# A hybrid SSM and latent-attention decoder layer: attention's weight splits and gates on GpSimd, weights loaded two ahead, and three moves around them

## The chip, the cores and the metric

The kernel runs on one NeuronCore of a Trainium2 chip. The metric is the device time in microseconds (us) of one execution; the median of several runs counts. Five engines work side by side, each through its own queue in order: TensorE (PE: matmuls, and the loads of their stationary operand, PEld), VectorE (DVE), ScalarE (ACT), GpSimd (POOL) and SyncE (SP, which only starts DMAs here). They wait for one another through semaphores.

## The reference, cut to what matters

One layer for 512 tokens of width 1024. Parallel head groups read the same normalised input through one input projection, one output projection mixes them, and an expert mixer (PEER) follows:

```python
proj = h @ w_in
z, xbc, dt_raw, q_lat, kv_lat, k_pe = jnp.split(proj, ...)
xbc = jax.nn.silu(causal_dwconv(xbc, conv_w, conv_b))
...
y_ssm = rms_norm(y.reshape(B, S, SSM_WIDTH) * jax.nn.silu(z), ssm_norm_g)
y_mla = mla_heads(q_lat, kv_lat, k_pe, cos, sin, q_norm_g, w_q_b, kv_norm_g, w_kv_b)
mix = jnp.concatenate([y_ssm, y_mla], axis=-1) @ w_out
...
h = layer_norm(DEEPNORM_ALPHA * h + mix, ln_mix_g, ln_mix_b)
ffn = peer(h, w_query, sub_keys, u_table, v_table)
```

The SSM heads (16, Mamba-2) work in chunks with decays exp(a_cum[l] - a_cum[s]). The latent attention has 8 heads of 128 unrotated and 64 rotated dimensions, and is causal. PEER picks 16 of 16384 experts for each token and head.

## The kernel before, in words

**Precision and the weight stream.** Nearly every product is made of three fast matmuls: each operand is split into a high part (rounded) and a low part (the rest), and `mm3` (L71 to L74) adds high by high (L72), high by low (L73) and low by high (L74). The weights come through one `Stream` called `win` (L80 to L127, made in L263): a list of items in the order of use, each at most 128 x 1024. `loads` starts the DMA of an item on SP into one of three raw buffers (tile `wir`); `his` makes the high part on ACT (L109, `wih`); `splits` makes the low part by a subtraction (L119, `wil`) on the engine that `lo_on[0]` names at that moment, and then asks for the raw load three items on. `get(n)` sees to it that items up to n + `win.la` are split: `la` is how many weights ahead the stream runs. There are three buffers of each part. Engines take their instructions in the order in which this program issues them, so where a split is issued decides what stands behind it.

**Stages.** (1) Input layer norm: statistics on DVE, normalising on ACT and DVE, transposes on PE (L311) into the eight tiles `PS8`, from which ACT and DVE make the split input HH and HL (L317 to L322). (2) Input projection, 18 column blocks (L592 to L616 and L657 to L669), and behind it the convolutions: `conv_a` (taps on DVE, L376 to L378), `conv_b` (Silu on ACT, L387), `conv_c` (transposes on PE, L396, and evacuation on ACT, L401). `ssd_a` (L478) makes eight exponentials of decays on ACT (L482) and multiplies them on DVE by the chunk's products (L483); `ssd_y` (L512) uses them and `xdt` (L494) in matmuls (L518). The list `work` (L618) lays the remaining SSM steps behind the later column blocks and the z projection (L672 on). (3) Attention, below. (4) The output projection for three token blocks (L1218 on), the mixing layer norm, the query projection (L953) with the top-16 searches on DVE, during which `lo_on[0]` is GpSimd, and the expert stage to the end.

**Attention (L857 to L901).** Ahead of the loop: `q_pe(0)` and `qk_nope(0)` in halves, then two halves of `chain(qk_nope(1), v_proj(0))`; a half ends at a `yield`. `q_pe` (L727) projects the rotated dimensions of a pair of heads: 9 matmuls, evacuation to `qx` on ACT (L734), a split of the next item, `yield`; then the permuting matmul (L738), the rotation on DVE (`rope`, L578 to L580), its halves (L742, L743) and four DMAs on GpSimd's queue (L746). `qk_nope` and `v_proj` (L770, L749) have two halves each and ask for the next split after a half. The loop has 39 steps; step st works for head st // 4 and query block st % 4: `p_scale` (two steps late; DVE L818, or ACT L816 for the longer rows of heads below 7), `scores` (PE, and the maximum on DVE, L800), `p_tr` (six steps late: transposes on PE, L827, evacuated as two halves by ACT, L721, and DVE, L722), one half of the projections (`next(g)`), from step 28 the output projection of the fourth token block (`w_out_step`, one item a step), `p_exp` (ACT, L808), `gate` in steps 1, 3, 5 and 7, and `p_v` (seven steps late). `gate(c, 1)` multiplies 512 columns of the SSM output by silu(z) on DVE (L541) and squares them on ACT (L543); `gate(c, 0)` runs earlier, from `work`. `win.la` is 0 in the loop up to step 27, so that only the explicit `win.splits(cnt[0] + 1)` run ahead; 1 from step 28; 2 once the output projection's first step has been issued.

Of the kernel before, what the change touches and what calls it, by code (L numbers as in the profile page):

```python
# [17 lines left out]
AF = mybir.ActivationFunctionType  # L18
OP = mybir.AluOpType
# [6 lines left out]
NB = 4  # L26
# [3 lines left out]
SCALE = 192.0 ** -0.5  # L30
# [23 lines left out]
def tile_block(ctx: ExitStack, tc: tile.TileContext, I, out):  # L54
    nc = tc.nc
    ctx.enter_context(tc.manual_schedule())
    V, A, T, G = nc.vector, nc.scalar, nc.tensor, nc.gpsimd
# [83 lines left out]
    def sqrt_rs(p, v, shape, tag, eps):  # L141
        h, q, y, a = (p.tile(shape, F32, name=tag + n) for n in "hqya")
        A.activation(q, v, AF.Sqrt, bias=eps)
        V.tensor_scalar(h, v, EPS, -0.5, op0=OP.add, op1=OP.mult)
        V.reciprocal(y, q)
        V.tensor_tensor(a, y, y, op=OP.mult)
        V.tensor_tensor(a, a, h, op=OP.mult)
        V.scalar_tensor_tensor(y, a, 1.5, y, op0=OP.add, op1=OP.mult)
        return y
# [76 lines left out]
    zt = zx.tile([128, NB, D], F32, name="zt")  # L226
    xs = [zx.tile([128, NB, 512], F32, name=f"xs{e}") for e in range(2)]
# [7 lines left out]
    ones = wk.tile([128, 128], F32, name="ones")  # L235
# [12 lines left out]
    lo_on = [V]  # L248
# [14 lines left out]
    win = Stream(wst, "wi", items, [128, 1024], raw=3, la=2, lo=lambda n: lo_on[0])  # L263
    cnt = [0]
# [22 lines left out]
    w0 = lnp.tile([128, 1], F32, name="w0")  # L287
    A.activation(w0, ones[:, 0:1], AF.Sqrt, bias=eps)
    PS8 = [pa() if k < 4 else pb() for k in range(8)]
    for p in range(2):  # L290
        bs = slice(2 * p, 2 * p + 2)
        for b in (2 * p, 2 * p + 1):
            st6 = lnp.tile([128, 2, 6], F32, name="st6", bufs=2)
            for i in range(2):
                V.bn_stats(st6[:, i], XH[:, b, i * 512:(i + 1) * 512])
            V.bn_aggr(mv4[:, b], st6.rearrange("p a b -> p (a b)"))
        nm = lnp.tile([128, 2], F32, name="nm", bufs=2)
        rs = sqrt_rs(lnp, mv4[:, bs, 1], [128, 2], f"l{p}", eps)
        V.scalar_tensor_tensor(nm, mv4[:, bs, 0], -1.0, rs, op0=OP.mult, op1=OP.mult)
        if p:  # L300
            win.his(1)
        for j, cs, act in (((0, slice(0, D), 1), (1, slice(0, D), 1)) if p == 0 else
                           ((0, slice(0, D), 0), (1, slice(0, 512), 1), (1, slice(512, D), 0))):
            t = XH[:, 2 * p + j, cs]
            if act:
                A.activation(t, t, AF.Identity, bias=nm[:, j:j + 1], scale=rs[:, j:j + 1])
            else:
                V.tensor_scalar(t, t, rs[:, j:j + 1], nm[:, j:j + 1], op0=OP.mult, op1=OP.add)
        for k in range(8):
            for b in (2 * p, 2 * p + 1):  # L310
                T.transpose(PS8[k][:, b * 128:(b + 1) * 128], XH[:, b, k * 128:(k + 1) * 128], ident)  # L311
    win.his(2)
    win.splits(1)
    for k in range(8):
        ht = lnp.tile([128, S], F32, name="ht", bufs=3)
        pl, pg = PAR[:, P_LB + k:P_LB + k + 1], PAR[:, P_LG + k:P_LG + k + 1]
        A.activation(ht, PS8[k], AF.Identity, bias=pl, scale=pg)  # L317
        if k % 2:
            A.activation(HH[:, k], PS8[k], AF.Identity, bias=pl, scale=pg)
        else:  # L320
# [37 lines left out]
    def proj(i):  # L358
        if i < 2:
            return two[i]  # L360
        hl = item()
        ps = pa()
        for k in range(8):
            proj_k(ps, hl, k)
        return ps
# [24 lines left out]
    def conv_c(i):  # L390
        o = co.pop(i)
        if i in (3, 4):
            return
        ps = pb()
        for c in range(NB):
            T.transpose(ps[:, c * 128:(c + 1) * 128], o[:, c * 128:(c + 1) * 128], ident)  # L396
        pv = ps.rearrange("p (c t) -> p c t", c=NB)
        if i <= 2:
            A.activation(btok[:, :, i - 1, :], pv, AF.Copy)
        else:  # L400
            A.activation(xs[(i - 5) // 4][:, :, (i - 5) % 4 * 128:((i - 5) % 4 + 1) * 128], pv, AF.Copy)  # L401
# [76 lines left out]
    def ssd_a(c, g):  # L478
        de = de_[c * 2 + g]
        for h in range(8):  # L480
            hh = g * 8 + h
            A.activation(de[:, h], de[:, h], AF.Exp, bias=nac[:, c, hh:hh + 1])  # L482
        V.tensor_tensor(de, de, SD["cb"][:, g:g + 1].to_broadcast([128, 8, 128]), op=OP.mult)  # L483

    def ssd_m(c, g):
        de = de_[c * 2 + g]
        V.tensor_tensor(de, de, ntm[:, None, :].to_broadcast([128, 8, 128]), op=OP.add)
# [38 lines left out]
    def ssd_s(c):  # L526
# [9 lines left out]
                A.activation(nxt[:, g * 512:(g + 1) * 512], pS, AF.Copy)  # L536
        prev[0] = nxt

    def gate(c, e):
        es = slice(e * 512, (e + 1) * 512)  # L540
        V.tensor_tensor(xs[e][:, c], xs[e][:, c], zt[:, c, es], op=OP.mult)  # L541
        t = wk.tile([128, S], F32, name="co", bufs=2) if e == 0 else ml.tile([128, S], F32, name="rp")
        A.activation(t, xs[e][:, c], AF.Square, accum_out=ssq[:, c, e:e + 1])  # L543

# [47 lines left out]
    for i in range(13):  # L592
        ps = proj(i)
        if i == 0:
            A.activation(kd[0:80], ps[0:80], AF.Copy)
        else:
            conv_a(i, ps)
        if i >= 2:
            conv_b(i - 1)
        if i >= 5:  # L600
            conv_c(i - 2)
        if i in (4, 5):
            conv_c(i - 3)
        if i in (2, 4, 6, 7, 9):
            next(dp)
        if i == 3:
            k_rope()
        if i == 11:
            ssd_m(0, 0)
        if i == 12:  # L610
            ssd_cb(0)
            ssd_m(0, 1)
            ssd_a(0, 0)
    conv_b(12)
    conv_c(11)
    ssd_a(0, 1)  # L616

    work = {0: [(conv_c, 12), (ssd_x, 0), (ssd_cb, 1), (ssd_m, 1, 0)],  # L618
# [38 lines left out]
    for i in range(13, 18):  # L657
        ps = proj(i)
# [68 lines left out]
    def q_pe(p):  # L727
        wh, wl = item()
        ps = pp()
        for k in range(3):  # L730
            ks = slice(k * 128, k * 128 + 128)
            mm3(ps, wh[:, ks], wl[:, ks], qlh[:, k], qll[:, k], k == 0, k == 2)
        qx = ml.tile([128, S], F32, name="qx")
        A.activation(qx, ps, AF.Copy, scale=SCALE)  # L734
        win.splits(cnt[0] + 1)
        yield
        pr = pp()
        T.matmul(pr, C[:, C_PQ:C_PQ + 128], qx, start=True, stop=True)  # L738
        a = rope(ml, qx, pr, "rp", 1)
        q2 = [ml.tile([128, S], F32R, name=f"q2{e}", bufs=2) for e in range(2)]  # L740
        qp = [ml.tile([128, S], F32R, name="qp" + n) for n in "hl"]
        A.activation(qp[0], a, AF.Copy)  # L742
        V.tensor_tensor(qp[1], a, qp[0], op=OP.subtract)  # L743
        for e in range(2):
            for x in (e, 1 - e):
                G.dma_start(q2[e][x * 64:x * 64 + 64], qp[e ^ x][e * 64:e * 64 + 64])  # L746
            QP[2 * p + e] = q2[e]
# [110 lines left out]
    for g in (gq, gk, gq, gk, gk):  # L858
        next(g, None)
    g = chain(qk_nope(1, pq=pt), v_proj(0))  # L860
    for _ in range(2):
        next(g)
    acc3 = {}
    win.la = 0
    for st in range(39):
        h, q = divmod(st, 4)
        if st == 28:
            win.la = 1
        if q == 0 and h:
            g = iter(())  # L870
            if h < 7:
                g = chain(qk_nope(h + 1), v_proj(h // 2)) if h % 2 == 0 else chain(q_pe(h // 2 + 1), qk_nope(h + 1))
        if 1 < st < 34:
            p_scale((st - 2) // 4, (st - 2) % 4)
        if st < 32:
            scores(h, q)
        if 6 <= st < 38:
            p_tr((st - 6) // 4, (st - 6) % 4)
        if GST[3] + 10 <= st < GST[3] + 18:
            y_tr(st - GST[3] - 10)  # L880
        next(g, None)
        if st >= 28:
            if st == 28:
                acc3 = {(3, e): pu() for e in range(2)}
            if st < 36:
                w_out_step(acc3, (3,), st - 28)
            elif st == 37:
                w_out_step(acc3, (3,), 8)
        if st < 32:
            p_exp(h, q)  # L890
        if st in GST:
            gate(GST.index(st), 1)
        if GST[3] < st <= GST[3] + 8:
            if st == GST[3] + 1:
                g2 = gate2()
            next(g2)
        if st == GST[3] + 8:
            ZH = zx.tile([128, NB, D], F32R, name="zt")
        if st >= 7:
            p_v((st - 7) // 4, (st - 7) % 4)  # L900
# [317 lines left out]
    acc = {(b, e): px() if b == 0 else pw() for b in range(3) for e in range(2)}  # L1218
    for k in range(10):
        w_out_step(acc, (0, 1, 2), k)  # L1220
        win.la = 2
        if k == 1:
            V.memset(one, 1.0)
            V.memset(scl, 1.0)
            rows(ROW, 2)
            nc.sync.dma_start(ident, I["idn"])
            for b in range(3):
                load_h(b)
# [101 lines left out]
    for m in range(17):  # L1330
# [9 lines left out]
        while tm[1] < tm[0] + T_Q:  # L1340
            c = next(fill, None)
# [340 lines left out]
```

## Time and profile before

| what | us |
|---|---|
| median of 3 runs (lowest, highest) | 1615.43 (1614.64, 1615.7) |
| the profiled execution | 1614.06 |
| its span, first to last instruction | 1612.3 |
| PE busy in the span | 1580.4 |
| DVE busy | 1356.4 |
| ACT busy | 711.2 |
| POOL busy | 470.3 |

All times of the trace count from the span's start. In these times the start and layer norm end at about 17, the input projections and the SSM steps at 201, attention at 340, the output projection for three blocks at 400, and the expert stage runs to the end. A group's row gives line, engine, operation, what is written from what is read, shapes and count, busy time and mean ns of one, then the idle time of the engine just before them and what ended it. A wait row gives who waited for whom, in total, how often, and the longest. The chain of waits is the work that ended last, followed back from the end: start, length, what. The end of a matmul is modelled, so PE's busy time is an upper bound.

### The profile page before, as it was taken

Reading aid. Unit: us, or ns where it says so; the run is one execution under the profiler, and the core shown is the slowest. Engines: PE = TensorE matmul, PEld = TensorE weight load, DVE = VectorE, ACT = ScalarE, POOL = GpSimd, SP = SyncE. Lnnn points to the kernel's source line nnn. Section 1 sums busy time; section 2 is a strip of 40 time slices with the busy share of each in tenths; the row PEclk is TensorE's granted clock in tenths of the full one; section 3 lists DMA queues with packets and bytes.
Section 4 is the critical chain, followed back from the end, with each engine's and each line's share of the span. In section 5 each row is a group of like instructions: output and inputs, shape, how many; then the busy total and the mean of one; then the engine's idle time right before and its main releaser. Section 6 shows DMA issues by size and latency. Waiting matters only on the chain.

```text
span 1612.3 us, 23768 instructions
## 1 busy us (share of the span) xinstructions
PE 1580.4 (98%) x8643; PEld 1391.4 (86%) x8643; DVE 1356.4 (84%) x2548; ACT 711.2 (44%) x1236; POOL 470.3 (29%) x340
## 2 busy tenths in 40 slices
PE   7999999999999999999999999999999999999997
PEld 5877878778888999999999999999999999888886
DVE  8979667746799999999488888888889888999877
ACT  5574467632433445556444333333334333333332
POOL 0000010000133223100045555555555555644400
PEclk9999999999999999999999999999999999999999
DMA  6242122374332458777689999999999999999973
GB/s 247 97 153 92 46 71 57 110 239 153 122 100 85 127 183 328 285 256 250 210 311 369 343 343 343 362 347 343 350 348 346 352 344 361 357 346 347 342 221 125
DMA packets 152254, 395.43 MB, mean 245 GB/s; under 512 B 12776, under 2 KB 65720, under 8 KB 150344
## 3 DMA queue, kind: packets, MB, share of 16 engines
q1 hardware_dynamic: 104952, 213.19, 39.3%
q0 software_dynamic: 43584, 155.29, 26.4%
q10 hardware_dynamic: 3600, 25.43, 4.2%
q8 instruction: 68, 1.11, 0.3%
q14 instruction: 50, 0.41, 0.1%
HBM read 359.99 MB, written 31.78 MB: 243 GB/s over the span
## 4 chain that ended last, share of the span: by engine, by line
PE 81%; DVE 13%; ACT 3%; issue 1%; DMA 1%; ACTq 0%; DVEq 0%; POOL 0%
PE va L1429 11%; PE va L1433 11%; PE va L1430 10%; PE pu L72 10%; PE pu L73 10%; PE pu L74 10%; PE pa L73 3%; PE pa L74 3%; PE pa L72 3%; DVE t L987 1%; PE pw L73 1%; PE pw L74 1%; DVE wil L119 1%; PE pw L72 1%; PE pw L1189 1%; PE pw L1190 1%
## 5 line engine op out<-in xcount | busy, mean ns | idle before, releaser
L109 ACT ACTIVATE wih<-wir 128x1024 fp32r<-128x1024 f32 (+2 forms) x269 | 278.0, 1034 | 299.9 <-DMA wir<-ut 104.5
L119 DVE TENSOR_TENSOR wil<-wir,wih 128x1024 fp32r<-128x1024 f32 (+1 forms) x254 | 302.4, 1191 | 102.6 <-ACT wih L109 56.9
L74 PE MATMUL pu<-XTH,wil 128*128 128x368 f32 x1008 | 331.8, 329 | 1.0 <-DVE wil L119 0.9
L72 PE MATMUL pu<-XTH,wih 128*128 128x368 f32 x904 | 299.9, 332 | 0.3 <-ACT act L1271 0.3
L73 PE MATMUL pu<-XTL,wih 128*128 128x368 f32 x904 | 296.8, 328 | 0.0
L1430 PE MATMUL va<-wil,Ph 128*128 128x512 f32 x726 | 282.7, 389 | 0.0
L1467 POOL DMA_INDIRECT row<-u,ix x128 | 185.3, 1448 | 250.8 <-DVE row L1478 128.6
L1467 POOL DMA_INDIRECT row<-v,ix x128 | 188.5, 1472 | 174.8 <-DVE ac L1484 149.2
L74 PEld LDWEIGHTS pu<-XTH,wil 128*128 128x128 f32 x1008 | 189.1, 188 | 1.7 <-DVE wil L119 1.6
L72 PEld LDWEIGHTS pu<-XTH,wih 128*128 128x128 f32 x904 | 169.7, 188 | 3.4 <-ACT act L1271 0.5
L73 PEld LDWEIGHTS pu<-XTL,wih 128*128 128x128 f32 x904 | 169.5, 188 | 2.9
L1429 PE MATMUL va<-wih,Ph 128*128 128x512 f32 x432 | 168.5, 390 | 0.0
L1484 DVE SCALAR_TENSOR_TENSOR ac<-row,hd,ac 128x1024 f32<-128x1024 f32 x128 | 164.1, 1282 | 3.2 <-DMA row<-v,ix 1.0
L1430 PEld LDWEIGHTS va<-wil,Ph 128*128 128x128 f32 x726 | 136.2, 188 | 25.9
L1478 DVE SCALAR_TENSOR_TENSOR row<-row,x 128x1024 f32<-128x1024 f32 x128 | 150.1, 1220 | 1.0 <-DMA row<-u,ix 0.9
L109 ACT ACTIVATE wihx<-wir 128x1024 fp32r<-128x1024 f32 x67 | 71.1, 1062 | 154.2 <-DMA wir<-v 132.4
L1433 PE MATMUL va<-wih,Pl 128*128 128x512 f32 x432 | 133.4, 390 | 0.0
L1271 ACT ACTIVATE act<-pu 128x368 f32<-128x368 f32 x126 | 59.9, 475 | 165.4 <-PE pu L74 165.2
L1429 PE MATMUL va<-wihx,Ph 128*128 128x512 f32 x294 | 114.8, 391 | 0.0
L119 DVE TENSOR_TENSOR wil<-wir,wihx 128x1024 fp32r<-128x1024 f32 x62 | 75.8, 1223 | 43.2 <-issue 32.5
L1433 PEld LDWEIGHTS va<-wih,Pl 128*128 128x128 f32 x432 | 81.1, 188 | 17.3
L1429 PEld LDWEIGHTS va<-wih,Ph 128*128 128x128 f32 x432 | 81.2, 188 | 15.7
(494 smaller groups left out, 3064.7 us busy)
## 6 DMA issues: line engine op xcount, KB each, us to landing
wir<-ut SPq DMA_DIRECT2D x128, 512.0 KB, 6.2
wir<-v SPq DMA_DIRECT2D x128, 512.0 KB, 6.6
gsp<-stg ACTq DMA_DIRECT2D x12, 1920.0 KB, 7.5
gt<-gsp SPq DMA_DIRECT2D x30, 768.0 KB, 10.2
wir<-wo SPq DMA_DIRECT2D x26, 512.0 KB, 4.1
wir<-wf SPq DMA_DIRECT2D x18, 512.0 KB, 3.3
wir<-wqr SPq DMA_DIRECT2D x16, 512.0 KB, 3.6
de<-acd POOLq DMA_DIRECT2D x8, 512.0 KB, 5.1
```

Of the source, the lines that this page charges most:

```text
L72: T.matmul(ps, lh, rh, start=start, stop=False)
L73: T.matmul(ps, lh, rl, start=False, stop=False)
L74: T.matmul(ps, ll, rh, start=False, stop=stop)
L109: A.activation(h, r, AF.Copy)
L119: self.lo(n).tensor_tensor(l, r, h, op=OP.subtract)
L1271: A.activation(ACT[c][:, :NU], ps, AF.Gelu)
L1429: T.matmul(va[b][e], Ph[:, bs], h[:, cs], start=c == 0, stop=False)
L1430: T.matmul(va[b][e], Ph[:, bs], l[:, cs], start=False, stop=False)
L1433: T.matmul(va[b][e], Pl[:, bs], h[:, cs], start=False, stop=c == 127)
L1467: G.indirect_dma_start(out=R[s], out_offset=None, in_=I["u"] if s < 128 else I["v"], in_offset=bass.IndirectOffsetOnAxis(ap=ix[:, s % 128: ...
L1478: V.scalar_tensor_tensor(r, r, 1.0, x3, op0=OP.mult, op1=OP.mult, accum_out=hd[:, s:s + 1])
L1484: V.scalar_tensor_tensor(ac, r, hd[:, s - 128:s - 127], ac, op0=OP.mult, op1=OP.add)
```

## The change

1. 28 matmuls of 128 x 128 ones into the last of the eight `PS8` tiles, ahead of the first transposes.
2. The SSM decays' first eight exponentials, `ssd_a(0, 0)`, are issued after the last convolution's Silu instead of before it.
3. The multiplication of `gate(c, 1)` goes to GpSimd; all four are issued ahead of the attention loop. The squares on ACT stay where they were.
4. `q_pe` evacuates `qx` on DVE for the pairs after the first.
5. A third half, the first of `v_proj(0)`, is issued ahead of the loop.
6. The low parts of weights are made on GpSimd from the loop's beginning to step 34, on DVE from step 35.
7. Weights run two ahead from step 28 (at step 27 two items are asked for), and stay so into the output projection.

```diff
     PS8 = [pa() if k < 4 else pb() for k in range(8)]
+    for _ in range(28):
+        T.matmul(PS8[7][:, 0:128], ones, ones, start=True, stop=True)
     for p in range(2):
...
+    def gate_mul(c, e, eng):
+        eng.tensor_tensor(xs[e][:, c], xs[e][:, c], zt[:, c, e * 512:(e + 1) * 512], op=OP.mult)
+
     def gate(c, e):
-        es = slice(e * 512, (e + 1) * 512)
-        V.tensor_tensor(xs[e][:, c], xs[e][:, c], zt[:, c, es], op=OP.mult)
+        if e == 0:
+            gate_mul(c, e, V)
...
             ssd_m(0, 1)
-            ssd_a(0, 0)
     conv_b(12)
     conv_c(11)
+    ssd_a(0, 0)
     ssd_a(0, 1)
...
         qx = ml.tile([128, S], F32, name="qx")
-        A.activation(qx, ps, AF.Copy, scale=SCALE)
+        if p:
+            V.tensor_scalar(qx, ps, SCALE, None, op0=OP.mult)
+        else:
+            A.activation(qx, ps, AF.Copy, scale=SCALE)
...
     g = chain(qk_nope(1, pq=pt), v_proj(0))
-    for _ in range(2):
+    for _ in range(3):
         next(g)
+    for c in range(NB):
+        gate_mul(c, 1, G)
     acc3 = {}
     win.la = 0
+    lo_on[0] = G
     for st in range(39):
         h, q = divmod(st, 4)
         if st == 28:
-            win.la = 1
+            win.la = 2
+        if st == 35:
+            lo_on[0] = V
...
         next(g, None)
+        if st == 27:
+            win.splits(cnt[0] + 2)
...
         w_out_step(acc, (0, 1, 2), k)
-        win.la = 2
```

## The prediction, made before the changed kernel was run

> **What bounds the kernel now.** I read first how busy each engine is by stage (columns: stage, its length, then busy time and instructions of PE, PEld, DVE, ACT, POOL, granted clock, DMA share, GB/s), and beside it one matmul group of the page (count, busy, mean ns, idle before).
> ```profile
> 201.00:340.00 139.00, 130.43 (x740) 106.89 (x739) 103.39 (x221) 92.14 (x201) 8.19 (x16) 1.00 0.34 96
> 590.00:1590.00 1000.00, 999.69 (x5663) 903.04 (x5662) 859.45 (x1061) 418.99 (x698) 401.38 (x280) 1.00 0.90 320
> ```
> ```profile
> L1430 PE MATMUL va<-wil,Ph 128*128 128x512 f32 x726 | 282.7, 389 | 0.0
> ```
> TensorE (PE) is the bound: in the long expert stage from 590 to 1590 it is idle 0.3 us. The change touches the start, the stretch around 100 us and the attention stage, 201 to 340, where PE is idle 8.6 of 139 us. All later work hangs on attention's result, so a microsecond won there moves the end by one. VectorE (DVE) works 103.4 us of that stage: not full, yet a queue in strict order, and PE waits for what stands late in it. So next I read who PE waits for (total us, times, longest), from 0 to 400.
> ```profile
> PE pa L311 <- ACT XH L306: 10.3, 2, 9.6
> PE pu L73 <- DVE wil L119: 1.7, 4, 0.8
> PE pt L827 <- DVE thl L722: 1.5, 2, 1.0
> PE pt L796 <- DMA q<-qpl: 1.4, 1, 1.4
> PE po L73 <- DVE thl L722: 1.0, 2, 0.7
> PE px L73 <- DVE wil L119: 0.8, 1, 0.8
> PE pt L567 <- DVE thl L722: 0.7, 1, 0.7
> PE pu L738 <- ACT qx L734: 0.7, 1, 0.7
> PE pb L518 <- PE pa L74: 0.7, 1, 0.7
> PE pb L396 <- ACT co L387: 0.7, 2, 0.4
> PE po L72 <- ACT thh L721: 0.7, 1, 0.7
> ```
> L311 is the start, L518 and L396 lie around 100 us. The other rows sum to 8.5, all of attention's idle time: 2.5 for split weights (wil), 3.9 for the probabilities' two halves (L721, L722), 1.4 for the rotated queries' DMA, 0.7 for qx. Ends of matmuls are modelled: 5663 in 999.69 us start 0.18 us apart, while 512 columns are given 389 ns. So each of these 14 waits can hide another 0.16, some 2.2 us in all (an estimate).
>
> **The change part by part.** *Warm-ups (after L289).* The transposes at the start:
> ```profile
> 12.29 1.92 PE L311 MATMUL pb<-ident,XH 128*128 128x128 f32 x8
> ...
> 15.20 1.04 PE L311 MATMUL pb<-ident,XH 128*128 128x128 f32 x8
> ```
> ```profile
> 14.67 1.45 ACT L317 ACTIVATE ht<-pa,PAR 128x512 f32<-128x512 f32 x2 [0.45 <-PE pa L311]
> ```
> Eight take 1.92 us, a later eight of the same 1.04: PE is slow at first. 28 such matmuls cost at most 28 x 0.24 = 6.7 us and wait for one memset, so they fit into PE's first wait of 9.6; if they didn't, each would push the transposes by 0.24. If the transposes then run fast, L317 starts earlier by its idle 0.45 at most, since ACT converts a weight until then. Bounds 0 and -0.45; I take **-0.4**, by the later eight. The Trainium skill (TensorE: Matmul & The Clock Gate, part 1) has the array at half clock again after an idle window of some 3.4 us. The gap here would be about 3, so by the page the gain could go either way, and no run here shows such a gap.
>
> *Exponentials behind the convolutions* (DVE's last convolution; then ACT's queue):
> ```profile
> 96.34 2.33 DVE L378 SCALAR_TENSOR_TENSOR ca<-cu,PAR,ca 128x512 f32<-128x512 f32 x3
> ```
> ```profile
> 97.01 1.28 ACT L482 ACT_TABLE_LOAD   x1
> 98.30 2.46 ACT L482 ACTIVATE de<-de,nac 128x128 f32<-128x128 f32 x8
> 100.77 1.28 ACT L387 ACT_TABLE_LOAD   x1
> ...
> 103.20 1.28 ACT L482 ACT_TABLE_LOAD   x1
> 104.50 2.46 ACT L482 ACTIVATE de<-de,nac 128x128 f32<-128x128 f32 x8
> ```
> Now: exp, Silu, exp, with three table loads. Afterwards Silu comes first and needs no load, but waits for its convolution, to 98.67. From the end of the second load to that of Silu and L401 are 103.20 - 102.05 = 1.15 us; with one load and sixteen exponentials, 98.67 + 1.15 + 1.28 + 4.92 = 106.0 against 106.96. The product and split that DVE owes to L518 come 0.9 sooner, and L396 finds its tile 3 us sooner. Bounds 0 and -1.4 (both rows); **-1.0**.
>
> *Third projection half in front.* Twelve 256-column matmuls move ahead of PE's wait for the query DMA; with their evacuation they are now steps 0's and 1's work, so nothing is added. At 0.18 us or less each they cover most of the 1.4. Bounds 0 and -1.4; **-1.2**.
>
> *Splits, gates and qx.* DVE's splits from 205 to 340, ACT's conversion ahead of them, GpSimd's rate in the query stage, and a landing time from the page:
> ```profile
> L119 DVE TENSOR_TENSOR wil<-wir,wih 128x1024 fp32r<-128x1024 f32 x14 | 17.2, 1226 | 6.4 <-ACT wih L109 6.1
> ```
> ```profile
> L119 DVE TENSOR_TENSOR wil<-wir,wih 128x640 fp32r<-128x640 f32 x6 | 4.9, 820 | 4.1 <-ACT wih L109 4.1
> ```
> ```profile
> L109 ACT ACTIVATE wih<-wir 128x1024 fp32r<-128x1024 f32 x14 | 14.8, 1054 | 3.6 <-DMA wir<-wo 2.2 <-DVE wil L119 1.3
> ```
> ```profile
> L119 POOL TENSOR_TENSOR wil<-wir,wih x15: 2385/2398/2415, 427.5 to 539.7; 128x1024 fp32r<-128x1024 f32 x15
> ```
> ```profile
> wir<-wo SPq DMA_DIRECT2D x26, 512.0 KB, 4.1
> ```
> Where they reach PE, from the chain of waits:
> ```profile
> 221.28 0.48 ACT qx L734
> 221.76 0.63 ACT wih L109
> ```
> ```profile
> 227.56 0.73 DVE wil L119
> 228.29 0.60 DVE xs L541
> ```
> Up to step 35, nine of the wide splits move (w_out 0 to 8), all six of 640 columns, three of 512 and two of 384 (by columns 0.66 and 0.49), and four gates (0.60): 11.0 + 4.9 + 2.0 + 1.0 + 2.4 = 21.3 us leave DVE. Three qx come to it, by columns 0.66 each: 19.3 net. On GpSimd, 2.40 for 1024 columns makes 1.50, 1.20, 0.90 and 1.20 a gate by columns (bounds: that, and 2.40 each): 21.6 + 9.0 + 3.6 + 1.8 + 4.8 = 41 us in 125. Its queue also issues the rotated queries' DMAs, in which it waits for ACT; the next weight behind them is used three steps later.
>
> *qx (0.7):* on DVE it no longer stands behind ACT's squares. But the weight that ACT converts behind it is used one step later; GpSimd takes 1.50 for it instead of 0.82 and starts 0.48 sooner, so it comes 0.2 later, three times. Bounds -0.7 and +2.0 (3 x 0.68); **-0.5**, nearer to the row. *Probabilities (3.9):* at 227.56 a split and a gate, 1.3 us, stand in DVE's queue ahead of a tile that PE wants; gone, that wait goes. Other waits have one split ahead, or softmax work alone. Bounds 0 and -3.9; **-2.5**. *w_out's weights (2.5):* two ahead takes most, but three raw buffers turn over in 4.1 + 1.05 + 2.40 = 7.55 us, and three fast steps now take 7.33, from the first to the last of four splits:
> ```profile
> 317.73 1.23 DVE L119 TENSOR_TENSOR wil<-wir,wih 128x1024 fp32r<-128x1024 f32 x1
> ...
> 325.06 1.23 DVE L119 TENSOR_TENSOR wil<-wir,wih 128x1024 fp32r<-128x1024 f32 x1 [0.26 <-ACT wih L109]
> ```
> Bounds 0 and -2.5; **-2.0**. Of the hidden 2.2 a third: **-0.8**.
>
> *The price: DVE and GpSimd at once.* The query stage has one place that shows it.
> ```profile
> L1003 DVE TENSOR_TENSOR cand<-tv x24: 199/254/1872, 442.0 to 543.2; 128x64 f32<-128x64 f32 x8, 128x96 f32<-128x96 f32 x8, 128x192 f32<-128x192 f32 x8
> ```
> ```profile
> 497.40 2.39 POOL L119 TENSOR_TENSOR wil<-wir,wih 128x1024 fp32r<-128x1024 f32 x1 [3.96 <-PE pw L74]
> 498.00 2.31 DVE L1003 TENSOR_TENSOR cand<-tv 128x64 f32<-128x64 f32 x3
> ```
> A sum of two SBUF operands whose median is 0.25 lasts up to 1.87: it stands until GpSimd's split ends. In attention the DVE operations on SBUF alone that remain are 18 scalings (L818), four of L560 and six of the rotations (L578, L743): 28. GpSimd is busy a third of the time, so 9 are hit, each by half a split, about 1.0: 9 us back on a queue that lost 19.3, of which PE waits for a tenth, as it now waits 8.5 us for a DVE stage of 103. Bounds 0 and +8.7 (28 hit, less 19.3); **+1.0**. The Trainium skill (SBUF — State Buffer, "Who interferes with whom") has such DVE instructions and a GpSimd instruction that reads SBUF exclude each other for a whole instruction. The row agrees; it is the rule against this change.
>
> Sum: -0.4 - 1.0 - 1.2 - 0.5 - 2.5 - 2.0 - 0.8 + 1.0 = **-7.4**. The profiled execution took 1614.06 (span 1612.3, and 1.8 around it): 1606.7. The median of the runs stands 1.37 above it, so I predict **1608.0**.
>
> **The rivals.** *All waits go:* -0.45 - 1.4 - 8.5 - 2.2 = -12.5, 1602.9. For it: DVE loses a fifth of its work. Against: some probability waits lie behind softmax work.
> *Late weights:* the three tight splits cost 0.68 each and qx stays in the way by what they take (+1.4 in all); the raw buffers keep w_out's waits (0); ACT, waiting in order for raw weights, halves the probabilities' gain (-1.2) and the hidden one (-0.4). With -2.6 from the first three terms and +1.0: -1.8, 1613.6. For it: 7.55 against 7.33, and DVE's idle 4.1 before the 640-wide splits: they start as soon as ACT is done, so nothing can be had by an earlier start. Against: two weights of lead. The Trainium skill (GPSIMD Engine Reference, 2.1) gives some 6 us for a first call after a kernel is loaded; that would hold the first gate, ACT's square behind it and this weight by a microsecond or two, and no row here shows such a load's price.
> *The lock* (slower): all 28 hit, since splits and scalings both follow ACT; DVE's queue is then 8.7 longer, and once its relief is spent PE waits for all of it: +8.7 - 2.6 = +6.1, 1621.5. It decides from about 19 hits; a third of 28 is 9.
>
> **How the numbers follow.** Forecast 0.58, all waits 0.14, late weights 0.19, the lock 0.09. A measurement can tell some 0.2% from no change, 3.2 us, so faster is below 1612.2: forecast, all waits and 0.02 of late weights, 0.74; same 0.17, slower 0.09. The range runs from under the second case to beyond the third, 1602.5 to 1616.0; the lock and the outer tails, under 0.2, stay out.
>
> **What would show it.** L796's DMA wait under 0.3; two table loads fewer between 95 and 107 and no L518 wait; eight transposes in about 1 us from the first; no waits of PE for wil; POOL some 41 us busier in attention, DVE 19 less plus the lock's share, which shows as longer L818 and L578; PE's idle 8.6 down to about 3. I am wrong if PE waits for wil on POOL, if the 28 lengthen by a microsecond each, or if idle time turns up after 340.

## The result, and the profile after

| | before | after |
|---|---|---|
| median, us (lowest, highest; 5 runs each, same chip) | 1614.64 (1613.85, 1615.7) | 1604.77 (1604.7, 1605.71) |
| the profiled execution | 1614.06 | 1604.7 |
| its span | 1612.3 | 1602.9 |

The ratio of the times is 0.9939, with a 95% interval of 0.9925 to 0.9954: 9.9 us faster, where 7.4 was forecast. (The time of before in the table ahead of the prediction comes from other runs.) As a time, 1608.0 was forecast: of the 3.2 us by which the measured one lies below it, some 2.5 are the change, and some 0.8 the kernel before, whose median was 1615.43 in the runs that the forecast started from. Lines of the kernel after stand 2 to 8 below those of before, and 14 in the expert stage: L313 is the old L311, L520 the old L518, L542 the gate product (L541), L552 and L565 the old L547 and L560, L727 the low part (L722), L740 and L742 qx on DVE and on ACT, L804 the old L796, L816 the exponential (L808), L826 the scaling (L818) and L835 the transposes of probabilities (L827).

To find where the time went I took the start of the same PE matmul in both traces and subtracted. Such a number is called a **shift** below. It falls in six steps:

| by (us in the trace of before) | shift | what lies there |
|---|---|---|
| 20 | -0.47 | first transposes |
| 200 | -1.30 | the exponentials near 100 us |
| 217.3 | -2.74 at the first scores, -1.32 behind them | third half in front: won, and given back |
| 224 | -2.07 | second pair's qx |
| 302 | -6.10 | the softmax steps |
| 340 | -9.50 | w_out's steps in the loop |
| 1590 | -9.36 | everything behind |

Attention in the changed kernel begins at about 200 and ends 9.5 sooner than before, at 330.5. Its busy time by engine (stage, length, then PE, PEld, DVE, ACT, POOL, granted clock, DMA share, GB/s):

```profile
201.00:332.00 131.00, 127.50 (x741) 107.03 (x741) 97.64 (x201) 89.67 (x194) 48.93 (x39) 1.00 0.37 105
```

PE is idle 3.5 us of it, where it was 8.6. Idle time fell by 5.1, yet the stage got 9.50 - 1.30 = 8.2 shorter, so 3.1 us stood in no idle row: by this subtraction they lay under the modelled ends of matmuls. The softmax steps and w_out's steps, the same work before and after:

```profile
224.00:302.00 78.00, 74.00 (x446) 61.92 (x444) 60.54 (x144) 53.88 (x127) 6.13 (x12) 1.00 0.27 70
302.00:340.00 38.00, 35.54 (x186) 28.35 (x186) 28.50 (x48) 24.62 (x44) 0.00 (x0) 1.00 0.55 171
```

```profile
221.93:295.90 73.97, 72.56 (x446) 61.67 (x444) 55.68 (x132) 52.92 (x124) 20.09 (x22) 1.00 0.27 71
295.90:330.50 34.60, 33.84 (x186) 28.44 (x186) 22.89 (x39) 24.87 (x44) 21.74 (x9) 1.00 0.61 184
```

PE's idle time falls from 4.0 to 1.4 and from 2.5 to 0.8, by 4.3 in all, and the two get 4.0 and 3.4 shorter. Whom PE still waits for, 0 to 400 us (total, times, longest):

```profile
PE pt L72 <- ACT P L816: 1.2, 1, 1.2
...
PE pt L572 <- DVE thl L727: 0.9, 1, 0.9
...
PE pt L835 <- DVE P L826: 0.4, 1, 0.4
PE pb L520 <- DVE xdt L496: 0.4, 1, 0.4
...
PE pb L398 <- ACT co L389: 0.4, 1, 0.4
PE pt L835 <- DVE thl L727: 0.4, 1, 0.4
PE pu L72 <- DVE vl L727: 0.3, 1, 0.3
...
PE po L73 <- DVE thl L727: 0.2, 1, 0.2
```

The reader is to see what is missing: the DMA wait of 1.4, qx's 0.7 and all the waits for split weights (wil, 2.5). Of 3.9 for the probabilities' halves (thl, thh), 0.9, 0.4 and 0.2 are left. New in attention are small rows for a scaling (0.4) and a value's low part (0.3), and the first: PE waits 1.2 for the softmax's exponential.

The start of PE's timeline (start, length, engine, line, operation, count, idle before):

```profile
1.07 9.25 PE L291 MATMUL pb<-ones 128*128 128x128 f32 x56 [1.07 <-DVE eps L285]
10.16 0.27 PE L313 MATMUL pa<-ident,XH 128*128 128x128 f32 x1
10.84 0.98 PE L313 MATMUL pa<-ident,XH 128*128 128x128 f32 x7 [0.41 <-ACT XH L308]
11.66 1.04 PE L313 MATMUL pb<-ident,XH 128*128 128x128 f32 x8
```

The 28 warm-ups are 56 records and take 9.25 us. They even push the first transpose from 9.62 to 10.16, which costs nothing, as the second has to wait for ACT until 10.84. From there all run at the fast rate. Near 100 us, ACT's timeline has one table load in place of three:

```profile
99.41 1.28 ACT L484 ACT_TABLE_LOAD   x1
100.70 4.80 ACT L484 ACTIVATE de<-de,nac 128x128 f32<-128x128 f32 x16
```

It ends at 105.5, where the working had 106.0 and the kernel before 106.96. GpSimd's groups in attention (count, busy, mean ns of one, idle before) and two of VectorE's:

```profile
L119 POOL TENSOR_TENSOR wil<-wir,wih 128x1024 fp32r<-128x1024 f32 x9 | 21.7, 2434 | 7.7 <-PE pt L805 5.0 <-ACT wih L109 2.7
L119 POOL TENSOR_TENSOR wil<-wir,wih 128x640 fp32r<-128x640 f32 x5 | 7.9, 1578 | 11.2 <-ACT wih L109 11.2
L542 POOL TENSOR_TENSOR xs<-xs,zt 128x512 f32<-128x512 f32 x4 | 5.0, 1306 | 0.1
```

```profile
L119 DVE TENSOR_TENSOR wil<-wir,wih 128x640 fp32r<-128x640 f32 x2 | 6.1, 3053 | 0.3 <-ACT wih L109 0.3
L826 DVE TENSOR_SCALAR P<-P,sm 128x256 f32<-128x256 f32 x8 | 3.6, 453 | 0.3
L565 DVE TENSOR_SCALAR xs<-xs,rqy 128x512 f32<-128x512 f32 x4 | 3.1, 776 | 0.0
```

Only five of the six 640-column splits went to GpSimd. The sixth stayed on VectorE, in a row with one from before 204 us, and their mean is 3053 ns where it had been 820. That is the most telling row of the trace, and it leads to the new wait. VectorE, GpSimd and ScalarE at that place:

```profile
209.43 5.28 DVE L119 TENSOR_TENSOR wil<-wir,wih 128x640 fp32r<-128x640 f32 x1
214.63 0.68 DVE L727 TENSOR_TENSOR vl<-pu,vh 128x512 fp32r<-128x512 f32 x1
215.24 0.28 DVE L808 TENSOR_REDUCE mx<-pt 128x1 f32<-128x128 f32 x1
```

```profile
208.98 5.04 POOL L542 TENSOR_TENSOR xs<-xs,zt 128x512 f32<-128x512 f32 x4
```

```profile
212.55 1.28 ACT L816 ACT_TABLE_LOAD   x1
215.55 0.37 ACT L816 ACTIVATE P<-pt,mx 128x128 f32<-128x128 f32 x1 [1.72 <-DVE mx L808]
```

One split of 640 columns stands for 5.28 us while GpSimd's four gate products run back to back, and ends 0.69 us after them (209.43 + 5.28 = 214.71, against 214.02). Behind it in VectorE's queue stand the value's low part and the first maximum; for the maximum waits the exponential, and for that PE.

### The profile page after: what moved, and what is told of

Read it like the earlier page. It is cut to its first block, busy times and chain, and to the rows that moved or that the text cites. A ratio compares the mean times of both kernels' runs of the same rounds, so it can differ in the third digit from the quotient of the medians.

```text
span 1602.9 us, 23887 instructions
## 1 busy us (share of the span) xinstructions
PE 1585.0 (99%) x8699; PEld 1398.6 (87%) x8699; DVE 1349.6 (84%) x2528; ACT 707.2 (44%) x1231; POOL 527.6 (33%) x363
## 4 chain that ended last, share of the span: by engine, by line
PE 89%; DVE 6%; ACT 3%; DMA 1%; issue 1%; DVEq 0%; ACTq 0%
PE pu L72 11%; PE va L1443 11%; PE va L1447 11%; PE va L1444 11%; PE pu L74 10%; PE pu L73 10%; PE pw L73 3%; PE pw L74 3%; PE pw L72 3%; PE pa L73 3%; PE pa L74 3%; PE pa L72 3%; PE pw L1204 1%; PE pw L1205 1%; PE pb L520 1%
## 5 line engine op out<-in xcount | busy, mean ns | idle before, releaser
L119 DVE TENSOR_TENSOR wil<-wir,wih 128x1024 fp32r<-128x1024 f32 (+1 forms) x235 | 288.3, 1227 | 94.4 <-ACT wih L109 63.7
L1481 POOL DMA_INDIRECT row<-u,ix x128 | 196.3, 1533 | 240.9 <-DVE row L1492 118.9
L1481 POOL DMA_INDIRECT row<-v,ix x128 | 194.1, 1516 | 167.5 <-DVE ac L1498 143.6
L119 POOL TENSOR_TENSOR wil<-wir,wih 128x1024 fp32r<-128x1024 f32 (+3 forms) x34 | 71.5, 2108 | 192.4 <-PE pw L74 140.9
L119 DVE TENSOR_TENSOR wil<-wir,wihx 128x1024 fp32r<-128x1024 f32 x62 | 75.8, 1222 | 34.3 <-issue 18.5
```

Of the source, the lines that this page charges most:

```text
L119: self.lo(n).tensor_tensor(l, r, h, op=OP.subtract)
L1481: G.indirect_dma_start(out=R[s], out_offset=None, in_=I["u"] if s < 128 else I["v"], in_offset=bass.IndirectOffsetOnAxis(ap=ix[:, s % 128: ...
```

## The experiments

The theory to be tested: **the lock** holds a VectorE instruction with two SBUF operands until GpSimd's run of instructions is over. In front of the loop it takes back what the third half wins. The rest of the gain is made by the engine that splits and by the lead of two weights. Rivals: the front's wait comes from the table load or from the order on ScalarE; the lead alone, or the engine alone, makes the gain behind it. Each kernel is the changed one with the edit given, except for `starts_alone`, which is the kernel before with two edits. Its runs are compared with the kernel before on the same chip (medians 1614.67, 1614.8 and 1614.73 in the three sets of runs).

Shifts against the kernel before, in the profiled executions:

```
                  200 us  217.4    224     302     340    1590   median us
after              -1.30  -1.34  -2.07   -6.10   -9.50   -9.36   1604.77
front_on_g         -1.33  -2.75  -3.50   -7.49  -10.67  -10.45   1605.25
front_again        -1.35  -2.77  -3.51   -7.52  -10.79  -11.08   1603.8
two_gates          -1.36  -2.78  -3.54   -6.06   -9.48   -8.89   1605.17 (one run)
two_halves         -1.32  -1.31  -1.61   -5.63   -8.99   -5.79   1605.24
gates_on_dve       -1.30  -2.69  -3.44   -5.86   -9.05   -9.08   1604.99
ahead_dve          -1.24  -1.28  -2.01   -4.78   -7.86   -6.58   1606.75
one_ahead          -1.33  -1.37  -2.09   -6.12   -0.05   +5.59   1614.13
qx_on_act          -1.30  -1.34  -1.17   -5.09   -7.84   -3.36   1605.69
starts_alone       -1.35  -1.30  -1.31   -1.35   -1.38   -0.92   1613.23
warm_14            -0.79  -0.80  -1.53   -5.49   -8.85   -8.15   1605.9 (one run)
front_and_scale    -1.36  -2.78  -3.53   -7.54  -10.96  -10.89   1603.2
```

Between 340 and 1590 some executions lose 1 to 6 us that others of the same kernel don't. In the profiled one of `two_halves` (1608.3, where the four others took 1605.02 to 1605.6) it is a wait in the expert stage:

```profile
PE va L1443 <- ACT Ph L1427: 2.1, 1, 2.1
```

So what an edit does to attention is read from the shift at 340, and its time from the median.

**front_on_g: the split in front goes to GpSimd.**

```diff
-    for _ in range(3):
+    for i in range(3):
+        if i == 2:
+            lo_on[0] = G
         next(g)
```

> Edit: the 640-column split that the third projection half asks for goes to GpSimd, ahead of its four gate products, and is not on VectorE any more. Theory (the lock): VectorE's 5.28 us instruction was held by GpSimd's four products that ran back to back; with the split in GpSimd's own queue no VectorE split stands there, vl and mx start some 4 us sooner, PE's wait of 1.2 us on ACT's exponential goes, and the third half keeps its 1.42 us: 1604.8 - 1.4 = 1603.4. Rival (late weight): the split takes 1.58 us on GpSimd instead of 0.82, the products and ACT's square come behind it, and the first query half or the first scores wait instead: 0 to -0.7, 1604.1 to 1604.8, and the row of vl and mx moves by less than 2 us.

Measured: 1605.25 us (1603.25 to 1610.36, six runs; ratio 0.9944, 0.9932 to 0.9956). VectorE and GpSimd at the place of the lock:

```profile
210.19 0.69 DVE L727 TENSOR_TENSOR vl<-pu,vh 128x512 fp32r<-128x512 f32 x1 [0.72 <-ACT vh L726]
210.80 0.28 DVE L808 TENSOR_REDUCE mx<-pt 128x1 f32<-128x128 f32 x1
212.55 0.69 DVE L727 TENSOR_TENSOR vl<-pu,vh 128x512 fp32r<-128x512 f32 x1 [1.47 <-ACT vh L726]
...
214.52 0.33 DVE L826 TENSOR_SCALAR P<-P,sm 128x128 f32<-128x128 f32 x1
```

```profile
209.45 1.56 POOL L119 TENSOR_TENSOR wil<-wir,wih 128x640 fp32r<-128x640 f32 x1 [0.59 <-ACT wih L109]
210.98 5.04 POOL L542 TENSOR_TENSOR xs<-xs,zt 128x512 f32<-128x512 f32 x4
```

The first maximum comes at 210.80 instead of 215.24, 4.4 sooner, as the lock theory said and the rival denied; PE's row of 1.2 is gone, and the shift at 224 is -3.50 against -2.07: 1.43 won. At 340 there are 1.17 of it left. The first vl stands beside GpSimd's split, the second, at 212.55, beside the products. Both read PSUM and last 0.69 as ever: they are not held. The scaling at 214.52 has all its operands in SBUF and starts beside the third product; it ends at 214.85, 0.08 after that product and 1.2 before the fourth is over, so it isn't held for the run. The mechanism is shown for the split; the time, by these six runs, is not.

**front_again: the same kernel on another chip.**

> Edit: the kernel front_on_g once more, on a chip where two others are timed beside it. Theory (its trace keeps 1.1 to 1.2 of the 1.4 at the end, and executions near 1605.3 have a late wait of some 2 us that has nothing to do with the edit): the lowest executions stand at 1603.3 to 1603.6, the lowest of the three kernels without the other edit. Rival (the earlier start makes the late wait more frequent): half or more of the executions stand at 1605 or above again, and the median is no better than 1604.8.

Measured: 1603.8 us (1603.01 to 1605.14, five runs; ratio 0.9935, 0.9921 to 0.9948), shift -10.79 at 340. Of eleven executions in all, six lie between 1603.0 and 1603.8, four between 1605.1 and 1605.6, and one at 1610.36. The theory holds for six of them; why five are later isn't settled, since the two profiled ones are among the six.

**two_gates: two gate products in front instead of four.**

```diff
-        if e == 0:
+        if e == 0 or c > 1:
             gate_mul(c, e, V)
...
-    for c in range(NB):
+    for c in range(2):
         gate_mul(c, 1, G)
```

> Edit: two of the four gate products go to GpSimd in front, the other two to VectorE at their old places in the loop. Theory (VectorE's split is held until GpSimd's run of instructions is over): the row falls with the length of the run, from 5.28 to about 5.28 - 2 x 1.3 = 2.7 us, and PE's wait on ACT's exponential of 1.2 to 0. Rival (the two share the port and the split is merely slowed, by 5.28 / 0.82 = 6.4 while both run): the split does 2.6 / 6.4 = 0.4 of its work beside two products and the rest alone, 2.6 + 0.49 = 3.1 us; or the length has nothing to do with the products: 5.28 as before.

Measured:

```profile
209.38 2.82 DVE L119 TENSOR_TENSOR wil<-wir,wih 128x640 fp32r<-128x640 f32 x1
```

```profile
208.93 2.58 POOL L542 TENSOR_TENSOR xs<-xs,zt 128x512 f32<-128x512 f32 x2
```

2.82 instead of 5.28. More telling than the length is the end: VectorE's instruction ends at 212.20, 0.69 after GpSimd's run at 211.51, the same 0.69 as with four products. Had it been only slowed, more of it would have been done beside the longer run. It is held until the run is over, and is not let in between two instructions of the run. PE's 1.2 is gone here too (shift -3.54 at 224). Behind the front, though, this kernel wins only 2.5 up to 302, where the changed kernel wins 4.0; what is lost there is told under `gates_on_dve`.

Such a hold to the end of a run isn't found for every pair. Late in the changed kernel's attention VectorE scales probabilities, with one operand from SBUF, beside a run of splits:

```profile
311.32 2.18 DVE L826 TENSOR_SCALAR P<-P,sm 128x384 f32<-128x384 f32 x1
```

```profile
310.88 9.78 POOL L119 TENSOR_TENSOR wil<-wir,wih 128x1024 fp32r<-128x1024 f32 x4 [0.87 <-ACT wih L109]
```

The scaling ends at 313.50. One split takes 2.4, so it waited for the first of the four, to 313.3, and not for the run. The scaling at 214.52 in `front_on_g` was not held for the run either, and there GpSimd's run is the very one, four gate products without a wait, that holds the split in the changed kernel. So the difference seems to lie in the operation held: the split reads two tensors in SBUF, the scaling one. Why that should matter, and whether every operation on two such tensors stands for a whole run, no run here shows.

**two_halves: without the third half.**

```diff
-    for _ in range(3):
+    for _ in range(2):
```

> Edit: only two projection halves in front, as in the kernel before. Theory (the lock): the third half's 1.42 us are given back behind the scores, since the split that it asks for is held for 5.28 us; without it that split goes to GpSimd later, so both the gain and the loss go: 1604.8 within 0.3, with PE's idle of some 1.4 us ahead of the scores back and its wait of 1.2 us on ACT's exponential gone. Rival (the third half earns what was forecast, and the wait on the exponential comes from the order on ACT, the table load among it): +1.2 to +1.4, 1606.0 to 1606.2, with both waits there.

Measured: 1605.24 us (ratio 0.994, 0.9927 to 0.9953), 0.5 above the changed kernel; shift -8.99 at 340, 0.5 less. PE's waits in attention begin with:

```profile
PE pt L804 <- DMA q<-qpl: 1.4, 1, 1.4
```

The DMA wait is back and that for the exponential is gone, so the two change places: the third half brings 0.5 in the changed kernel, between the theory's 0 and the rival's 1.2 to 1.4, nearer to the theory, though outside its 0.3. It arises between 217.4 and 224, where the second pair's qx lies (-1.61 against -2.07); at 217.4 the shifts are the same (-1.31 and -1.34).

**gates_on_dve: the gate products back on VectorE.**

```diff
-        if e == 0:
-            gate_mul(c, e, V)
+        gate_mul(c, e, V)
...
-    for c in range(NB):
-        gate_mul(c, 1, G)
```

> Edit: the four gate products return to VectorE, each at its old place in the loop; splits stay on GpSimd. Theory (the lock): nothing runs on GpSimd beside the 640-column split in front, which takes 0.82 us instead of 5.28, so the front wins 1.4; VectorE has four products of 0.68 in the first steps of the softmax again, of which each may cost PE up to 0.7 where a tile of probabilities is due behind it: 1603.4 to 1606.2, likeliest 1604.2. Rival (the products, not the splits, were what PE waited for): the waits for probabilities come back as they were ahead of step 8, 1.3 us at 227.56 among them, and the front wins nothing: 1606 to 1607.

Measured: 1604.99 us (ratio 0.9943, 0.993 to 0.9956). The front wins its 1.4 (-3.44 at 224), and behind it the softmax steps win 2.4 up to 302, where the changed kernel wins 4.0. Among PE's waits stands

```profile
PE po L73 <- DVE thl L726: 1.0, 2, 0.9
```

The gate product's own 0.68 us is not the most of it. VectorE, GpSimd and PE at that place:

```profile
223.83 2.30 DVE L825 TENSOR_SCALAR P<-P,sm 128x128 f32<-128x128 f32 x1
...
226.53 0.67 DVE L726 TENSOR_TENSOR thl<-pt,thh 128x512 fp32r<-128x512 f32 x1
```

```profile
224.43 1.61 POOL L119 TENSOR_TENSOR wil<-wir,wih 128x640 fp32r<-128x640 f32 x1
```

```profile
227.25 0.50 PE L73 MATMUL po<-thl,vh 128*128 128x512 f32 x1 [0.89 <-DVE thl L726]
```

Behind a gate product, a scaling starts at 223.83 instead of 223.17 (`front_on_g`) and lasts 2.30 instead of 0.29: it stands until GpSimd's split has ended at 226.04, and the half that PE wants stands behind it. Some 1.1 of the 1.6 that the softmax steps lose against `front_on_g` lie at this one matmul. In `two_gates` the same scaling lasts 2.23.

Both theories were half right: gates on GpSimd are worth 1.6 behind the front, most of it because VectorE's work then keeps out of the way of that split, and cost 1.4 in it. In the changed kernel that part comes to nearly nothing; with the split moved (front_on_g) it is worth its 1.6.

**ahead_dve: all splits on VectorE, still two ahead.**

```diff
-    lo_on[0] = G
     for st in range(39):
```

> Edit: all splits return to VectorE; two weights ahead at the end, gate products on GpSimd, qx and the third half stay as in the changed kernel. Theory (the engine): 36 splits, some 17 us, stand among the softmax's work on VectorE again, so the waits for tiles of probabilities come back, 2 to 3 us of the 4.0 won between 226 and 302, while w_out's gain stays: 1606.8 to 1607.8. Rival (the lead): PE's waits were for weights one step ahead, and with two ahead it does not matter who makes them; with fewer GpSimd instructions beside them the lengthened VectorE operations get short as well: 1604.2 to 1605.2. In both, the 640-column split in front stays on VectorE and is held for some 5 us.

Measured: 1606.75 us (1605.91 to 1607.55; ratio 0.9947, 0.9933 to 0.9961), 2.0 above the changed kernel by the medians, 1.6 by the shift at 340. From 224 to 302 it wins 2.8 (4.0 with GpSimd), from 302 to 340 3.1 (3.4). The row that tells the difference:

```profile
PE pt L835 <- DVE thl L727: 1.2, 2, 1.0
```

The time is at the lower edge of the engine theory's range, but the wait that came back costs 1.2, not 2 to 3. The gain at w_out stays, as said.

**one_ahead: splits on GpSimd, one weight ahead from step 28.**

```diff
         if st == 28:
-            win.la = 2
+            win.la = 1
...
-        if st == 27:
-            win.splits(cnt[0] + 2)
...
+        win.la = 2
```

> Edit: w_out's weights one step ahead, as in the kernel before, but still split on GpSimd up to step 35. Theory (the lead makes w_out's gain): a split of 2.40 us and the conversion before it now lie in each step of 1.8 to 2 us, PE waits 1.3 us or more in each of seven steps: 1604.8 + 9 or more, 1614 or later, slower than splits on VectorE one ahead. Rival (the gain came from a freed VectorE, the lead is only spare): at most 3.4, the whole gain of that part, goes: 1604.8 to 1608.2.

Measured: 1614.13 us (1612.73 to 1619.65, eleven runs; ratio 0.9995, 0.9985 to 1.0004). The last line of the edit stands where the kernel before has it, in the output projection.

```profile
PE pu L73 <- POOL wil L119: 5.4, 6, 1.9
PE px L73 <- DVE wil L119: 0.7, 1, 0.7
```

At 302 us nothing differs (-6.12); at 340 the shift is -0.05, 9.45 behind the changed kernel. GpSimd's slower split costs that much as soon as it may not run ahead. The lead theory holds for w_out's steps. With `ahead_dve` the two roles are clear: at w_out the lead makes the gain and lets GpSimd be used; in the softmax steps the lead plays no part, and the engine makes 1.2 of the 4.0.

**qx_on_act: all four qx on ScalarE.**

```diff
-        if p:
+        if p < 0:
             V.tensor_scalar(qx, ps, SCALE, None, op0=OP.mult)
```

> Edit: all four qx products on ScalarE, as in the kernel before. Theory (each qx stands behind other ScalarE work): the shift of some 0.7 that stands at 222 to 226 goes, the other two pairs cost up to as much each, of which later waits take back most: 1605.3 to 1606.2, and PE's wait of 0.7 on ScalarE's qx is there again at 222. Rival (the gain at 222 is that of the split that left VectorE): within 0.3 of 1604.8.

Measured: 1605.69 us (1605.4 to 1610.69; ratio 0.9942, 0.9928 to 0.9957), 0.9 above; the shift at 224 is -1.17, so 0.9 are lost there, and 1.66 at 340.

```profile
PE pu L746 <- ACT qx L742: 1.0, 1, 1.0
PE pu L73 <- POOL wil L119: 0.7, 1, 0.7
...
PE pu L74 <- POOL wil L119: 0.3, 1, 0.3
```

The theory holds. There is one thing more: with qx on ScalarE, PE waits for weights from GpSimd as well. The 0.3 lies at 247.6, where ScalarE converts that weight behind the third pair's qx; the 0.7 lies in w_out's steps, and why it came there was not taken apart.

**starts_alone: two parts by themselves** (the warm-ups and `ssd_a(0, 0)` behind the convolutions, in the kernel before).

> Edit: the kernel before with the 28 warm-up matmuls and the exponentials behind the convolutions only. Theory (two gains that stand by themselves): -0.46 at the transposes and -0.84 in the chunk part, both kept to the end, -1.3: 1613.3. Rival (waits later in the span eat an earlier start, since DMAs or the softmax set the times there): the shift of 1.3 is there at 200 us and less than 0.5 of it at the end: 1614.1 or more.

Measured: 1613.23 us (1612.61 to 1614.91, eleven runs; ratio 0.9991, 0.9983 to 1.0) against 1614.67: 1.4 by the medians, 1.38 by the shift at 340. As the theory said: by the medians, the starts' gain reaches the end.

**warm_14: half the warm-ups.**

```diff
-    for _ in range(28):
+    for _ in range(14):
```

> Edit: 14 warm-up matmuls instead of 28, which end near 1.1 + 28 x 0.21 = 7.0 us, some 3 us ahead of the first transpose. Theory (PE is fast once it has been busy for some 5.5 us, and a gap of 3 us does not undo it): the first eight transposes take 1.0 us as in the changed kernel, no time is lost. Rival (14 are too few, or the gap undoes them): the first eight take 1.9 us as in the kernel before, and the shift of 0.46 at the transposes is gone.

Measured: one run, 1605.9 us; PE's timeline:

```profile
1.07 5.33 PE L291 MATMUL pb<-ones 128*128 128x128 f32 x28 [1.07 <-DVE eps L285]
9.69 0.45 PE L313 MATMUL pa<-ident,XH 128*128 128x128 f32 x1 [3.30 <-ACT XH L308]
10.74 1.76 PE L313 MATMUL pa<-ident,XH 128*128 128x128 f32 x7 [0.60 <-ACT XH L308]
12.29 1.92 PE L313 MATMUL pb<-ident,XH 128*128 128x128 f32 x8
```

The rival holds. The 14 are enough: their starts are 0.21 us apart up to 5.07 and 0.11 after. But then PE is idle for 3.30, and the transposes take 1.76 and 1.92 again; the granted clock from 10 to 13 us is 0.50:

```profile
10.00:13.00 3.00, 2.40 (x12) 2.26 (x12) 2.60 (x10) 2.47 (x4) 0.00 (x0) 0.50 0.98 385
```

The shift at 20 us is 0.00, and at 200 it is -0.79 instead of -1.30: the gain of the warm-ups is gone.

**front_and_scale: front_on_g, and the last head's long scalings on ScalarE.**

```diff
-        if qb > 1 and h < 7:
+        if qb > 1:
             A.activation(P[:, :n], P[:, :n], AF.Copy, scale=sm)
```

> Edit: the 640-column split in front on GpSimd, ahead of the gate products, and the last head's two long products of probabilities on ScalarE, as all other heads have them. Theory (the two lengthened VectorE products of some 2.1 us, at steps 32 and 33, hold PE by 0.4 to 0.6): the trace is 1.2 ahead of the changed kernel at 300 us and 1.6 to 1.8 ahead at 340; 1603.0 to 1603.2 where no late wait comes. Rival (ScalarE is the later engine there, with raw weights of w_out to convert): the 0.5 is lost again, or more: 1603.5 to 1604.2.

Measured: 1603.2 us (1603.05 to 1604.26, five runs; ratio 0.9931, 0.9918 to 0.9945). Of PE's waits in attention four are left: 0.9, 0.4 and 0.2 for the probabilities' halves and 0.3 for a value's low part. Neither the exponential (1.2) nor the scaling (0.4 in the changed kernel, 0.7 in `front_on_g`) is left among them. The shift at 340 is -10.96, 1.46 ahead of the changed kernel; the scalings' part of that is only 0.17 to 0.29 (against -10.79 and -10.67), less than the 0.4 to 0.6 expected. All five runs lie below the changed kernel's lowest (1604.7), so it is the fastest of all kernels run here, by 1.6 us against the changed one by the medians; the 95% intervals of the two ratios to before overlap, though, and the two were not timed side by side.

**gates_late: the kernel of front_and_scale once more** (its name does not tell its edit).

> Edit: the same kernel as front_and_scale, one look more, for its trace. Theory: no wait of PE behind 400 us that the changed kernel does not have, 1603.0 to 1603.2. Rival: the late wait of some 2 us, 1605.

Measured: 1603.72 us, shift -10.85 at 340 and -10.33 at 1590: no late wait of 2 us, half a microsecond lost in the expert stage. It is one execution, 0.5 above what the theory said.

## Why the prediction came out as it did, point by point

- **Warm-ups, -0.4: -0.47, for a reason that the working didn't have.** They were to end before 9.6, with a gap of about 3 us ahead of the transposes. They took 9.25 instead of at most 6.7, being 56 records, and left no gap. `warm_14` has the gap, 3.30, and loses the gain. So the step's doubt was the right one, and the size came out by luck: a miscount closed the gap. The Trainium skill (TensorE: Matmul & The Clock Gate, part 1) has the array at half clock after an idle window of some 3.4 us; the trace bears that out with one that is a little shorter, 3.30 idle and then a granted clock of 0.50.
- **Exponentials, -1.0: -0.83** (from -0.47 to -1.30), with the end on ACT 0.5 sooner than worked out. The waits shrank but did not go: PE still waits 0.4 at L520, for xdt, and 0.4 at L398, where 0.7 each had been and no L518 wait was to be left. `starts_alone` shows that both terms stand by themselves.
- **Third half, -1.2, and the lock, +1.0.** The half won 1.42, all of the DMA wait. The lock took it back at a place that was not on its list. The step that failed is the count of moved splits: "all six of 640 columns" were to go to GpSimd, but `lo_on` changes only behind the front, and the third half asks for one of them before that. On that split alone VectorE lost 5.28 - 0.82 = 4.46. On the 28 listed operations the forecast was 9 us of holding, 9 hits of 1.0. It was 6.1, in six hits, five of them scalings from 298 us on, where GpSimd's wide splits lie close together: the sixteen short scalings 0.7 and 0.8, the two long ones 1.8 and 1.6, L565 1.2, each by the difference of its mean to before; the rotations, none. PE paid 1.4 in front, and the long scalings 0.2 to 0.3 that last; with both mended, `front_and_scale` stands 1.46 ahead at 340. So the lock cost about 1.5 where +1.0 stood. PE paid a third of one instruction's hold, the one that stood ahead of a due maximum, and little of the rest; that this comes to an eighth of all 11.7 us of holding, near the tenth that was assumed, is luck. The Trainium skill (SBUF — State Buffer, "Who interferes with whom") has such instructions exclude each other for a whole instruction; the scaling at 311.32 agrees (2.18, to the end of one split), and the split goes beyond it, since it stood through four instructions (5.28) and through two (2.82).
- **qx, -0.5:** at the second pair -0.73 (from -1.34 to -2.07; without the third half, in `two_halves`, only -0.30), and `qx_on_act` puts all three pairs at 0.9 by the medians and 1.7 in the trace. The lower bound of -0.7 was too near.
- **Probabilities, -2.5, w_out, -2.0, and the hidden part, -0.8,** together -5.3, were -4.0 and -3.4, 7.4. This is the size that was most off, and the term that was mis-sized is the hidden part. Visible idle time fell by 2.6 and 1.7 in these steps, 4.3 where -2.5 and -2.0 stood, so the rows were read rightly. The hidden part was taken as a third of 2.2; it was 3.1, more than the whole 2.2 that was held possible. That bound was itself roughly worked: the list has 13 such waits, not 14, and 389 ns less 0.18 us is 0.21, not 0.16, which gives 2.1 to 2.7. A wait in the list is worth more than its row says. Of the causes, `ahead_dve` gives the engine 1.2 of the 4.0, `gates_on_dve` gives the gates 1.6, mostly by the one held scaling, and the remaining 1.2 was not taken apart; the parts need not add up. At w_out, `ahead_dve` keeps 3.1 of 3.4, so the lead makes it.
- **All waits go** (-12.5) was as near to the measured -9.9 as the forecast's -7.4. The trace decides between them: 3.5 of the 8.6 us of idle time stayed, so not all waits went.
- **Late weights** did not come true: in the changed kernel no row has PE waiting for wil on POOL, though the ring of raw buffers was worked out at 7.55 us against 7.33. `one_ahead` shows what the case would have looked like, and the 0.7 in `qx_on_act` that it was not far off. GpSimd took 1.58, 1.29 and 1.02 us for 640, 512 and 384 columns and 1.31 for a gate, within 0.12 of the rates assumed, and its 41 us were 40.5. The Trainium skill (GPSIMD Engine Reference, 2.1) has some 6 us for a first call after a kernel is loaded; nothing like it stands ahead of the first gate here, which starts 0.08 us after the DMA issue before it.
- **The lock as the slower case** needed 19 hits with PE paying for all. Six of the 28 were hit. More holding came than the 9 us of the forecast (11.7: 6.1 on the 28, and 4.5 and 1.1 on two others, L119 and the small sum at L552), but on a queue with slack PE pays only where a tile is due. The holding shows in VectorE's busy time: of the 19.3 that were to leave, 11.7 came back in this way and 0.8 as the split that stayed, which leaves 6.8; measured were 5.8 (103.4 to 97.6).

## What to carry to other kernels

Before work goes to GpSimd, list every VectorE instruction with SBUF operands that can stand beside it, by the place in the program where the engine is chosen and not by the stage it belongs to, and reckon that one on two SBUF operands can stand for a whole run of GpSimd instructions. A start that moves by 0.7 us can be enough to fall into such a hold (0.29 became 2.30). A slower engine can take over a stream if it is given a longer lead first: GpSimd's splits one ahead cost 9.5 us, two ahead nothing. Warm-up work for PE must reach up to the work it is meant for.

## What the runs showed of the hardware

- PE's slow phase at the start is not of fixed length: in twelve executions with 28 warm-ups their starts were 0.21 us apart for the first 2.9 to 5.9 us and 0.11 after that, and the slow phase in `warm_14` lasted 4.0.
- The granted clock of a short stretch can miss it. From 10 to 13 us the kernel before has 1.00 (the row below, columns as above), though its transposes start 0.21 us apart there; `warm_14`, at the same rate, has 0.50. The rate of the matmuls themselves is the safer sign.

```profile
10.00:13.00 3.00, 2.34 (x12) 2.26 (x12) 2.60 (x10) 2.47 (x4) 0.00 (x0) 1.00 0.95 371
```

- A held VectorE instruction shows no wait. It is listed as busy, 5.28 us long; only its mean beside the same shape elsewhere (820 ns) gives it away.
